# Storing the lower weight halves of block 0's projections in DRAM and loading them in the three later blocks

## The chip, the cores and the metric

The kernel runs on one core of a Trainium2 chip. The metric is the device time of one execution in microseconds; below that is the median of the runs shown. A profiled execution has its own time, which stands beside its span.

## The reference, cut to what matters

One hybrid decoder layer over 2048 tokens of width 1024 (float32), with 16 learned meta tokens ahead of them:

```
h    = rmsnorm(x, norm1_g)
proj = h @ w_in                       # all input projections at once
dq, dk, dv, dz, db, da, gq, gk, gv, gr, glr = split(proj)
o_dn  = gated_delta_chunked(conv+silu of dq, dk, dv, ...)   # 4 heads, chunk by chunk, a state is carried
o_gla = gla_chunked(gq, gk, gv, ...)                        # 4 heads, the same
x = x + concat(o_dn, o_gla gated and normed) @ w_out
x = x + square(relu(rmsnorm(x) @ w_up)) @ w_down
return rmsnorm(x)
```

What the change touches is `h @ w_in`, made once for each block of 512 tokens with the same `w_in`.

## The kernel before, in words

**Products of float32 from three passes.** An operand is split into an upper half `hi` (the value rounded to the matmul's own format, by ScalarE) and a lower half `lo = value - hi` (by VectorE or GpSimd). `mm3` (L116 to L120) then makes three matmuls into one PSUM bank: upper by upper (L118), and the two products of an upper and a lower half (L119, L120). Nothing is kept of a lower half between blocks: each block splits the same weights anew.

**A chunk of weights.** `wchunk` (L96) loads a raw chunk `wraw` of 128 x 2 x n from DRAM (L98, three buffers), casts it to `whi` on ScalarE (L102, two buffers) and subtracts to get `wlo` (L103, two buffers). In the projections the subtraction of chunks 1 and 2 of each group of four is on GpSimd, that of chunks 0 and 3 on VectorE. n is 512 for `wch` and 390 for `wtk`.

**The projections, `phase_a(b)`.** There are four blocks of 512 tokens (b = 0 to 3). A block has eight groups, in this order: `wtk` 0, `wch` 0 to 2 (keys, queries and values, with a convolution after each), `wch` 3, `wtk` 1 to 3. Each group has four chunks of 24 matmuls: 32 chunks and 768 matmuls a block, besides small products for the meta tokens in block 0. The tokens' operand comes from `xk` (L185), split into `hh` and `hl` (L113, L114). Results leave PSUM through VectorE and ScalarE and go to DRAM (`qkv_d`, `gla_d`, `gate_d`, `gv_d`).

**The scan.** `ahead(b)` runs at the middle of phase_a(b): four `dn_pre` (L481, each loads a `kqv` tile, three buffers) and `dn_inverse` (L559, a chain of small VectorE steps on `inv_v`, which goes through DRAM on both sides). `scan_chunk` carries the state: a GLA part (`gla`) and a delta part (`dn_levels`, `dn_rec`, which loads `kqv` as well). Scan chunks of block b stand between the projection matmuls of block b+1, so TensorE has independent work while a chain of the scan waits. Block 0 has no scan before it. After the projections come the output projection (`wo_block`) and the MLP (`layer1`, `layer2`), which the change doesn't touch.

**What sets the order.** The program is written once, and a scheduler with priorities orders the instructions of each engine; each engine then takes its own list strictly in order and waits on semaphores. All loads and stores are issued by one queue, SP's, in its order, so what waits there holds all behind it. A transfer also waits until the one that was issued eight before it has landed (the lanes DMAHW0 to DMAHW7 in the rows below). Pools fix how many buffers a name has; a load into a buffer waits for the last reader of what was there.

`k4` tiles (L72) are 4 KB a partition, four buffers, for statistics and decays.

Of the kernel before, what the change touches and what calls it, by code (L numbers as in the profile page):

```python
# [8 lines left out]
F32 = mybir.dt.float32  # L9
F32R = mybir.dt.float32r  # L10
I32 = mybir.dt.int32
AF = mybir.ActivationFunctionType
ALU = mybir.AluOpType
# [3 lines left out]
D = 1024  # L17
# [24 lines left out]
def hybrid_kernel(ctx: ExitStack, tc: tile.TileContext, I: dict, out: bass.AP):  # L42
    nc = tc.nc
    V, A, G, T = nc.vector, nc.scalar, nc.gpsimd, nc.tensor

    cp = ctx.enter_context(tc.tile_pool(name="const", bufs=1))
    dp = ctx.enter_context(tc.tile_pool(name="scratch", bufs=1, space=DRAM))
    mmp = ctx.enter_context(tc.tile_pool(name="mmp", bufs=4, space=PSUM))
    wp = ctx.enter_context(tc.tile_pool(name="wts", bufs=2))
    wstack = ctx.enter_context(ExitStack())  # L50
    wk = wstack.enter_context(tc.tile_pool(name="work", bufs=2))
# [11 lines left out]
    def mm(name):  # L63
        return mmp.tile([128, 512], F32, name=name, tag="mm")
# [5 lines left out]
        return wk.tile([128, 512], F32, name=name, tag="t512", bufs=4)  # L70

    def k4(name, q=wk):  # L72
        return q.tile([128, D], F32, name=name, tag="k4", bufs=4)

    def av(name, dt=F32, q=wk):
        return q.tile([128, TB + 4], dt, name=name, tag="av", bufs=8)
# [16 lines left out]
    mhalf = const("mhalf", [128, 16])  # L93
    G.memset(mhalf, -0.5)

    def wchunk(src, n, q=wp, eng=V):  # L96
        raw = wp.tile([128, 2, 512], F32, name="wraw", tag="wr", bufs=3)
        nc.sync.dma_start(out=raw[:, :, 0:n], in_=src)  # L98
        hi = q.tile([128, 2, 512], F32R, name="whi", tag="wh")
        lo = q.tile([128, 2, 512], F32R, name="wlo", tag="wl")  # L100
        with tc.high_priority(offset=HP):
            A.copy(out=hi[:, :, 0:n], in_=raw[:, :, 0:n])  # L102
            eng.tensor_tensor(  # L103
                out=lo[:, :, 0:n], in0=raw[:, :, 0:n], in1=hi[:, :, 0:n].bitcast(F32), op=ALU.subtract
            )
        return raw, hi, lo

    def split(src, hi, lo, scale=None):
# [23 lines left out]
    xs_d = [dp.tile([128, NK, TB], F32, name=f"xs_d{b}") for b in range(NB)]  # L132
    rb_d = [dp.tile([128, TB], F32, name=f"rb_d{b}") for b in range(NB)]
    sq_d = [dp.tile([128, 16, TB], F32, name=f"sq_d{i}") for i in range(7)]


    scan = ctx.enter_context(ExitStack())
    bps = scan.enter_context(tc.tile_pool(name="bps", bufs=4, space=PSUM))
    bp = scan.enter_context(tc.tile_pool(name="scan", bufs=1, side="right"))

    def ps(name):
        return bps.tile([128, 512], F32, name=name, tag="ps")
# [16 lines left out]
    def phase_a(b, kc, late=None, mid=None):  # L159
        convw, tails, g1, ealog, dtb, w2, gb, rmask = kc  # L160
        meta = b == 0
# [19 lines left out]
        def normless(k):  # L181

            if k not in hT:
                xk = t512("xk")
                nc.sync.dma_start(out=xk, in_=I["xT"][b, k])  # L185
                hT[k] = act("h")
                split(xk, *hT[k], g1[:, k : k + 1])
            return hT[k]
# [4 lines left out]
        if meta:  # L193
# [6 lines left out]
                out=hm[:, :, 0:NMETA], in0=hm[:, :, 0:NMETA], in1=g1.unsqueeze(2).broadcast_to([128, NK, NMETA]), op=ALU.mult  # L200
# [36 lines left out]
        def step(between):  # L237

            for job in list(stages):
                if between or not job[1]:  # L240
                    job[1] = next(job[0], None)
                    if job[1] is None:
                        stages.remove(job)

        def group(src, n, chan, evac, on_done, meta_n=0, on_meta=None, mid=None):
            banks = [mm("pa") for _ in range(4)]
            pm = ps("pmeta") if meta_n else None
            mh = meta_n // 2
            for kk in range(4):
                raw, wh, wl = wchunk(src[kk], n, eng=G if kk in (1, 2) else V)  # L250
                for j in range(4):
                    for k2 in range(2):
                        k = 2 * kk + k2
                        js = slice(j * 128, (j + 1) * 128)
                        h = normless(k)
                        w = (wh[:, k2, 0:n], wl[:, k2, 0:n])
                        if chan:
                            mm3(banks[j], [x[:, js] for x in w], h, k == 0, k == NK - 1)
                        else:
                            mm3(banks[j][:, 0:n], [x[:, js] for x in h], w, k == 0, k == NK - 1)  # L260
                step(False)
                for q in range(4 if meta_n else 0):
                    half, k2 = divmod(q, 2)
                    T.matmul(
                        pm[32 * q : 32 * q + 32, 0:mh],
                        lhsT=hm[:, 2 * kk + k2, :],
                        rhs=raw[:, k2, half * mh : (half + 1) * mh],
                        start=kk == 0,
                        stop=kk == 3,
                    )  # L270
            if mid is not None:
                mid()
            if meta_n:
                sb = k4("msb")
                V.tensor_copy(out=sb[:, 0:mh], in_=pm[:, 0:mh])
                po = ps("pmeta2")
                if chan:
                    for j in range(4):
                        c0 = j % 2 * 128
                        T.matmul(  # L280
                            po[:, j * NMETA : (j + 1) * NMETA], lhsT=sb[:, c0 : c0 + 128], rhs=eq[:, j // 2, :], start=True, stop=True
                        )
                else:
                    for half in range(2):
                        T.matmul(po[0:NMETA, half * mh : (half + 1) * mh], lhsT=eq[:, half, :], rhs=sb[:, 0:mh], start=True, stop=True)
                on_meta(po)
            st = [evac(j, banks[j]) for j in range(4)]
            step(True)
            for j in range(4):
                on_done(j, st[j])  # L290
# [190 lines left out]
    def dn_pre(c):  # L481
# [3 lines left out]
        gcb = b2k("gcb", "gcb", 2)  # L485
        if c is not None:
            b, t = divmod(c, 4)
            kqv = bp.tile([128, 12, 128], F32, name="kqv", tag="kqv", bufs=3)
            nc.sync.dma_start(out=kqv[:, 0:8, :], in_=qkv_d[b][:, 0:8, t * 128 : (t + 1) * 128])
            load_gcb(gcb, c)  # L490
            bt, gc = beta[b][:, t, :], gct[b][:, t, :]
        else:
            kqv = kqv_m
            load_gcb(gcb, c)
            bt, gc = beta_m[:, 0, :], gct_m[:, 0, :]
# [25 lines left out]
        if c is not None:  # L521
# [13 lines left out]
            out=gm[:p, :, 0:p], in0=gcb[:p, :, 0:p], in1=madd[:p, 0:p].unsqueeze(1).broadcast_to([p, 4, p]), op=ALU.add  # L535
# [7 lines left out]
        for h in range(4):  # L543
            V.scalar_tensor_tensor(
                out=U[:p, h, 0:p], in0=h4(pkk)[:p, h, 0:p], scalar=nbrk2[:p, h : h + 1], in1=gm[:p, h, 0:p], op0=ALU.mult, op1=ALU.mult
# [108 lines left out]
    def dn_rec(r, gate, mix, first):  # L654
# [2 lines left out]
        load_gcb(gcb, c)  # L657
        if c is not None:
            b, t = divmod(c, 4)
            kqv = bp.tile([128, 12, 128], F32, name="kqv", tag="kqv", bufs=3)  # L660
            nc.sync.dma_start(out=kqv, in_=qkv_d[b][:, :, t * 128 : (t + 1) * 128])
            at, kdt = b2k("at", "at", 1), b2k("kdt", "kdt", 1)
            nc.sync.dma_start(out=at, in_=at_d[c])
            nc.sync.dma_start(out=kdt, in_=kdt_d[c])
        else:
            kqv, kdt = kqv_m, r["kdt"]
# [31 lines left out]
        else:  # L698
            for h in range(4):
                V.scalar_tensor_tensor(  # L700
                    out=S[:, h, :], in0=S[:, h, :], scalar=egc[:, h, p - 1 : p], in1=h4(pu)[:, h, :], op0=ALU.mult, op1=ALU.add
# [761 lines left out]
```

## Time and profile before

| | before |
|---|---|
| median of 3 runs | 2676.49 us (2676.47 to 2682.16) |
| profiled execution: its time, its span | 2689.82 us, 2688.0 us |
| TensorE busy | 2468.2 us (92%) |
| VectorE busy | 1900.8 us (71%) |
| ScalarE busy | 1145.8 us (43%) |
| GpSimd busy | 498.0 us (19%) |
| moved by DMA | 477.81 MB, 178 GB/s on the mean |
| mean granted TensorE clock | 0.954 |

Rows of the profile name an engine, a line of the kernel, the operation, and the tiles out<-in. "PE" is TensorE, "PEld" its weight loads, "DVE" VectorE, "ACT" ScalarE, "POOL" GpSimd, "SPq" the queue that issues transfers. In the table of stretches each row is a stretch of the span in microseconds with its length, the busy time of each engine and its number of instructions in brackets, then the granted TensorE clock, the mean busy share of the 16 DMA engines and GB/s. In a row of waits stand the waiting engine and line, what it waited for, the microseconds in total, the number of times and the longest.

### The profile page before, as it was taken

How to read it: one execution, taken by the hardware profiler on the slowest of the kernel's cores; microseconds unless marked ns; L12 is line 12 of the kernel's file. 1: busy time of each engine (PE TensorE's matmuls, PEld its weight loads, DVE VectorE, ACT ScalarE, POOL GpSimd, SP SyncE). 2: the span in 40 equal slices, each digit the busy share in tenths (PEclk: the TensorE clock that was granted, in tenths of full speed). 3: DMA queues.
4: the chain of work that ended last, by engine and by line, in shares of the span. 5: the costliest groups of instructions: out<-in, count | busy, mean ns of one | idle time of the engine just before them, and what ended most of it. 6: DMA issues, size and time to landing. Idle time of an engine off the chain costs nothing.

```text
span 2688.0 us, 36763 instructions
## 1 busy us (share of the span) xinstructions
PE 2468.2 (92%) x12810; PEld 2034.4 (76%) x12810; DVE 1900.8 (71%) x3405; ACT 1145.8 (43%) x2243; POOL 498.0 (19%) x380
## 2 busy tenths in 40 slices
PE   8958999899989997996999999999969999899997
PEld 6747878777877786775778887778757888788776
DVE  4857788679787968667666666677778666557765
ACT  3334444434543454334444454443354444444433
POOL 2122233333332341111011110000111111100002
PEclk9979999899999998997999999999989999999998
DMA  5266546745674468653444447667527444656644
GB/s 174 91 197 193 160 153 198 226 151 177 200 218 148 160 202 288 197 166 108 147 141 159 143 147 264 206 217 226 165 91 249 166 144 151 209 187 210 214 136 134
DMA packets 304074, 477.81 MB, mean 178 GB/s; under 512 B 44545, under 2 KB 147537, under 8 KB 303889
## 3 DMA queue, kind: packets, MB, share of 16 engines
q1 hardware_dynamic: 303888, 475.48, 54.6%
q8 instruction: 100, 1.64, 0.2%
q14 instruction: 86, 0.70, 0.1%
HBM read 341.12 MB, written 134.26 MB: 177 GB/s over the span
## 4 chain that ended last, share of the span: by engine, by line
PE 52%; DVE 7%; DMA 3%; issue 1%; ACT 1%; SPq 1%; POOL 0%; DVEq 0%; POOLq 0%; ACTq 0%
PE p L119 15%; PE p L118 15%; PE p L120 15%; PE pc L120 2%; PE pc L118 2%; PE pc L119 1%; DMA br<-sq_d 1%; DVE bl L983 1%; DVE b L954 0%; DVE wlo L103 0%; DMA gcb<-gcr_d 0%; DMA xr<-xs_d 0%; DMA gl<-gla_d 0%; SPq L592 0%; DMA mixk<-mix_d 0%
## 5 line engine op out<-in xcount | busy, mean ns | idle before, releaser
L119 PE MATMUL p<-bl,w7h 128*128 128x512 f32 x832 | 325.5, 401 | 9.3 <-DVE bl L983 9.3
L120 PE MATMUL p<-bh,w7l 128*128 128x512 f32 x832 | 320.1, 398 | 0.0
L982 ACT CAST w7h<-s 128x1024 fp32r<-128x1024 f32 (+1 forms) x128 | 120.5, 942 | 346.6 <-PE p L119 287.9
L118 PE MATMUL p<-bh,w7h 128*128 128x512 f32 x832 | 228.9, 403 | 14.9 <-ACT bh L982 12.7
L102 ACT CAST whi<-wraw 128x1024 fp32r<-128x1024 f32 (+1 forms) x160 | 154.6, 967 | 205.9 <-PE pa L119 77.8
L118 PE MATMUL pa<-hh,whi 128*128 128x512 f32 x512 | 210.6, 412 | 9.9 <-DVE craw L424 4.6
L983 DVE TENSOR_TENSOR w7l<-s,w7h 128x1024 fp32r<-128x1024 f32 (+1 forms) x128 | 140.0, 1094 | 94.8 <-ACT w7h L982 90.5
L103 POOL TENSOR_TENSOR wlo<-wraw,whi 128x780 fp32r<-128x780 f32 (+1 forms) x64 | 144.2, 2254 | 338.5 <-ACT whi L102 281.4
L119 PE MATMUL pa<-hl,whi 128*128 128x512 f32 x512 | 206.6, 404 | 0.0
L118 PEld LDWEIGHTS p<-bh,w7h 128*128 128x128 f32 x832 | 159.4, 192 | 54.8 <-ACT bh L982 13.9
L120 PE MATMUL pa<-hh,wlo 128*128 128x512 f32 x512 | 196.4, 404 | 1.9 <-DVE wlo L103 1.5
L119 PEld LDWEIGHTS p<-bl,w7h 128*128 128x128 f32 x832 | 158.4, 190 | 49.5 <-DVE bl L983 11.5
L983 DVE TENSOR_TENSOR w7l<-w,w7h 128x1024 fp32r<-128x1024 f32 (+1 forms) x96 | 102.0, 1062 | 128.1 <-ACT w7h L982 124.3
L118 PE MATMUL pa<-whi,hh 128*128 128x390 f32 x512 | 173.7, 361 | 17.9 <-ACT hh L113 17.5
L119 PE MATMUL pa<-wlo,hh 128*128 128x390 f32 x512 | 182.2, 357 | 6.3 <-DVE wlo L103 4.2
L120 PEld LDWEIGHTS p<-bh,w7l 128*128 128x128 f32 x832 | 157.9, 190 | 37.8
L120 PE MATMUL pa<-whi,hl 128*128 128x390 f32 x512 | 177.0, 350 | 0.0
L983 DVE TENSOR_TENSOR bl<-br,bh 128x1024 fp32r<-128x1024 f32 (+2 forms) x144 | 149.2, 1038 | 32.1 <-ACT bh L982 31.9
L982 ACT CAST bh<-br 128x1024 fp32r<-128x1024 f32 (+2 forms) x144 | 123.2, 855 | 85.0 <-PE p L120 48.1
L103 DVE TENSOR_TENSOR wlo<-wraw,whi 128x1024 fp32r<-128x1024 f32 (+1 forms) x96 | 114.4, 1192 | 62.1 <-ACT whi L102 61.6
L1083 POOL TENSOR_TENSOR q<-r 128x512 f32<-128x512 f32 x32 | 58.5, 1829 | 521.4 <-ACT r L1082 479.2
L891 POOL TENSOR_TENSOR tot<-tot,sqk 128x512 f32<-128x512 f32 (+1 forms) x28 | 37.9, 1354 | 625.7 <-ACT sqk L890 624.5
(380 smaller groups left out, 6232.7 us busy)
## 6 DMA issues: line engine op xcount, KB each, us to landing
br<-sq_d SPq DMA_DIRECT2D x208, 256.0 KB
w<-in_dn_dram SPq DMA_DIRECT2D x96, 512.0 KB
wraw<-in_wch_dram SPq DMA_DIRECT2D x64, 512.0 KB
w<-in_up_dram SPq DMA_DIRECT2D x64, 512.0 KB
sq_d<-q SPq DMA_DIRECT2D x128, 256.0 KB
wraw<-in_wtk_dram SPq DMA_DIRECT2D x64, 390.0 KB
sq_d<-c SPq DMA_DIRECT2D x96, 256.0 KB
wraw<-in_wo_dram SPq DMA_DIRECT2D x32, 512.0 KB
```

The costliest lines, as they stand in the source:

```text
L102: A.copy(out=hi[:, :, 0:n], in_=raw[:, :, 0:n])
L103: eng.tensor_tensor(out=lo[:, :, 0:n], in0=raw[:, :, 0:n], in1=hi[:, :, 0:n].bitcast(F32), op=ALU.subtract)
L118: T.matmul(o, lhsT=ah, rhs=bh, start=first, stop=False)
L119: T.matmul(o, lhsT=ah, rhs=bl, start=False, stop=False)
L120: T.matmul(o, lhsT=al, rhs=bh, start=False, stop=last)
L891: eng.tensor_tensor(out=tot, in0=tot, in1=sq, op=ALU.add)
L982: A.copy(out=hi, in_=x)
L983: V.tensor_tensor(out=lo, in0=x, in1=hi.bitcast(F32), op=ALU.subtract)
L1083: G.tensor_tensor(out=q12, in0=u, in1=r5, op=ALU.add)
```

## The change

In block 0 each lower half is made as before and then also stored to DRAM, in 32 new tiles `lo_d`. In blocks 1 to 3 the subtraction is gone and `wlo` is loaded from `lo_d`; the raw chunk is still loaded, because ScalarE still casts the upper half from it. A third buffer for `wlo` (tag `wl3`) is used by every third chunk of a block. Two pools give up room for it: `k4` goes from four buffers to three and `kqv` from three to two. All transfers are issued by SP.

The numbers: 32 stores in block 0 and 96 loads in blocks 1 to 3, half of them of 512 KB and half of 390 KB; 48 subtractions go from VectorE and 48 from GpSimd.

```
-        return q.tile([128, D], F32, name=name, tag="k4", bufs=4)
+        return q.tile([128, D], F32, name=name, tag="k4", bufs=3)
...
-    def wchunk(src, n, q=wp, eng=V):
+    def wchunk(src, n, q=wp, eng=V, save=None, saved=None, third=False):
         raw = wp.tile([128, 2, 512], F32, name="wraw", tag="wr", bufs=3)
         nc.sync.dma_start(out=raw[:, :, 0:n], in_=src)
         hi = q.tile([128, 2, 512], F32R, name="whi", tag="wh")
-        lo = q.tile([128, 2, 512], F32R, name="wlo", tag="wl")
+        if third:
+            lo = wk.tile([128, 2, 512], F32R, name="wlo", tag="wl3", bufs=1)
+        else:
+            lo = q.tile([128, 2, 512], F32R, name="wlo", tag="wl")
+        if saved is not None:
+            nc.sync.dma_start(out=lo[:, :, 0:n].bitcast(F32), in_=saved[:, :, 0:n])
         with tc.high_priority(offset=HP):
             A.copy(out=hi[:, :, 0:n], in_=raw[:, :, 0:n])
-            eng.tensor_tensor(
-                out=lo[:, :, 0:n], in0=raw[:, :, 0:n], in1=hi[:, :, 0:n].bitcast(F32), op=ALU.subtract
-            )
+            if saved is None:
+                eng.tensor_tensor(
+                    out=lo[:, :, 0:n], in0=raw[:, :, 0:n], in1=hi[:, :, 0:n].bitcast(F32), op=ALU.subtract
+                )
+        if save is not None:
+            nc.sync.dma_start(out=save[:, :, 0:n], in_=lo[:, :, 0:n].bitcast(F32))
         return raw, hi, lo
...
+    lo_d = [[dp.tile([128, 2, 512], F32, name=f"lo_d{i}{k}") for k in range(4)] for i in range(8)]
...
             for kk in range(4):
-                raw, wh, wl = wchunk(src[kk], n, eng=G if kk in (1, 2) else V)
+                d = lo_d[gi][kk]
+                raw, wh, wl = wchunk(src[kk], n, eng=G if kk in (1, 2) else V, **{"save" if meta else "saved": d}, third=(4 * gi + kk) % 3 == 2)
...
-            kqv = bp.tile([128, 12, 128], F32, name="kqv", tag="kqv", bufs=3)
+            kqv = bp.tile([128, 12, 128], F32, name="kqv", tag="kqv", bufs=2)
```

`gi` counts the groups of a block from 0 to 7, and the last hunk stands in both `dn_pre` and `dn_rec`.

The rows of an engine's list below are in its order; what stands in brackets is what the instruction waits for (a DMAHW lane is a transfer issued earlier). In the changed kernel L99 is the raw load, L106 the load of a lower half, L114 its store, L196 the load of `xk`, L375 the store of the gates and L505 the load of `kqv` in `dn_pre`.

GpSimd in block 1, between the scan's products `kg` and `qg` and the next ones, before:

```order
L677 TENSOR_TENSOR kg<-kqv,egc 128x512 [waits Activation_49]
L678 TENSOR_TENSOR qg<-kqv,egc 128x512
L103 TENSOR_TENSOR wlo<-wraw,whi 128x1024 [waits DMAHW5_49,PE_49,Activation_49]
L103 TENSOR_TENSOR wlo<-wraw,whi 128x1024 [waits DVE_49,PE_49,DMAHW3_49,Activation_49,Pool_49]
L103 TENSOR_TENSOR wlo<-wraw,whi 128x1024 [waits DVE_49,DMAHW4_49,PE_49,Activation_49]
L90 TENSOR_TENSOR f_r<-f_u,mhalf 128x4 [waits DVE_49]
L766 TENSOR_TENSOR kd<-gl,dl 128x2x64 [waits DMAHW0_49,PE_49]
```

And now:

```order
L90 TENSOR_TENSOR f_r<-f_u,mhalf 128x4 [waits DVE_49]
L693 TENSOR_TENSOR kg<-kqv,egc 128x512 [waits Activation_49]
L694 TENSOR_TENSOR qg<-kqv,egc 128x512
L90 TENSOR_TENSOR f_r<-f_u,mhalf 128x4 [waits DVE_49,Pool_49]
L782 TENSOR_TENSOR kd<-gl,dl 128x2x64 [waits DMAHW3_49,PE_49]
```

The scan's own small steps (`f_r`, `kd`) now follow one another with no subtraction between them.

SP at the start of block 1, where the first `xk` of the block is loaded, before:

```order
L98 DMA wraw<-in_wtk_dram 128x2x390 [waits Pool_49] x2
L98 DMA wraw<-in_wtk_dram 128x2x390 [waits DVE_49]
L98 DMA wraw<-in_wtk_dram 128x2x390 [waits DMAHW7_49,DMAHW2_49,DVE_49]
L359 DMA gate_d_82<-gth 128x390 [waits DMAHW3_49,DVE_49]
L359 DMA gate_d_82<-gth 128x390 [waits DMAHW4_49,DVE_49]
L359 DMA gate_d_82<-gth 128x390 [waits DMAHW5_49,DVE_49]
L847 DMA gate<-gate_d_82 128x512 [waits DMAHW6_49,DMAHW3_49]
L185 DMA xk<-in_xT_dram 128x512
```

And now:

```order
L106 DMA wlo<-lo_d_163 128x2x390 [waits DMAHW2_49,DMAHW0_49,PE_49]
L99 DMA wraw<-in_wtk_dram 128x2x390 [waits DMAHW1_49,Activation_49]
L375 DMA gate_d_82<-gth 128x390 [waits DVE_49]
L106 DMA wlo<-lo_d_164 128x2x390 [waits DMAHW3_49,PE_49]
L106 DMA wlo<-lo_d_165 128x2x390 [waits DMAHW4_49]
L375 DMA gate_d_82<-gth 128x390 [waits DMAHW5_49,DVE_49]
L375 DMA gate_d_82<-gth 128x390 [waits DMAHW6_49,DVE_49]
L375 DMA gate_d_82<-gth 128x390 [waits DMAHW7_49,DVE_49]
L99 DMA wraw<-in_wtk_dram 128x2x390 [waits DMAHW0_49,Activation_49]
L99 DMA wraw<-in_wch_dram 128x1024 [waits DMAHW1_49,Activation_49]
L863 DMA gate<-gate_d_82 128x512 [waits DMAHW2_49]
L196 DMA xk<-in_xT_dram 128x512 [waits DMAHW3_49]
```

A raw load now waits only for ScalarE's cast, no longer for a subtraction. A load of a lower half waits for TensorE, and two of them and two raw loads have come between the first gate store of this stretch and the load of `xk`.

SP in the middle of block 0, where the four `dn_pre` load their `kqv`, before:

```order
L489 DMA kqv<-qkv_d_74 128x8x128 [waits DMAHW3_49]
L489 DMA kqv<-qkv_d_74 128x8x128 [waits DMAHW4_49]
L440 DMA qkv_d_74<-cy 128x512 [waits DMAHW5_49,DVE_49]
L440 DMA qkv_d_74<-cy 128x512 [waits DVE_49]
L477 DMA gcb<-gcr_d_90 128x512 [waits Pool_49]
L489 DMA kqv<-qkv_d_74 128x8x128 [waits DMAHW2_49,PE_49]
```

And now:

```order
L505 DMA kqv<-qkv_d_74 128x8x128 [waits DMAHW4_49,PE_49]
L493 DMA gcb<-gcr_d_90 128x512 [waits Pool_49]
L570 DMA u_d_99<-U 128x512 [waits DMAHW5_49,DVE_49]
L570 DMA at_d_115<-at 128x512 [waits DMAHW6_49,DVE_49]
L570 DMA kdt_d_132<-kdt 128x512 [waits DMAHW7_49,DVE_49]
L456 DMA qkv_d_74<-cy 128x512 [waits DMAHW0_49,DVE_49]
L505 DMA kqv<-qkv_d_74 128x8x128 [waits DMAHW1_49,PE_49]
```

Before, one of the four `kqv` loads waited for TensorE; now the last two do, and the last one also stands behind stores of the first `dn_pre`'s results.

## The prediction on record

> **What bounds the kernel now.** I read the page's busy times first, then the table of stretches with cuts between the blocks, then TensorE's waits in blocks 1 to 3, which alone lose the subtractions. The page's first rows:
>
> ```profile
> span 2688.0 us, 36763 instructions
> PE 2468.2 (92%) x12810; PEld 2034.4 (76%) x12810; DVE 1900.8 (71%) x3405; ACT 1145.8 (43%) x2243; POOL 498.0 (19%) x380
> ```
>
> The stretches are block 0, the projections of blocks 1, 2 and 3 with the scan among them, and the end of the scan with most of the output projection; the MLP follows:
>
> ```profile
> core 0: us, PE busy (x) PEld busy (x) DVE busy (x) ACT busy (x) POOL busy (x), PEclk, DMA share, GB/s
> 0.00:215.00 215.00, 175.79 (x918) 136.77 (x919) 137.94 (x327) 74.87 (x190) 49.46 (x39) 0.89 0.48 156
> 215.00:475.00 260.00, 240.84 (x1478) 210.40 (x1476) 201.65 (x451) 115.80 (x297) 83.68 (x67) 0.95 0.58 178
> 475.00:735.00 260.00, 237.18 (x1504) 203.51 (x1504) 205.83 (x457) 110.15 (x287) 85.44 (x64) 0.95 0.59 184
> 735.00:1015.00 280.00, 259.95 (x1707) 224.62 (x1705) 222.69 (x502) 122.68 (x340) 94.40 (x72) 0.98 0.60 184
> 1015.00:1320.00 305.00, 255.50 (x1515) 209.34 (x1514) 208.93 (x434) 119.25 (x250) 39.50 (x41) 0.89 0.56 183
> ```
>
> TensorE is busy 738.0 of 800 us in blocks 1 to 3 (the sum of three rows), so all that any change to the other engines can give back there is 62 us of idle time, and what the clock loses around it: the granted clock is 0.96 on the mean of the three, some 32 us of full speed. VectorE is busy 630.2 of 800 us (79%), GpSimd 263.5 (33%). What TensorE waited for between 215 and 1015 us:
>
> ```profile
> PE pa L118 <- ACT hh L113: 11.2, 1, 11.2
> PE py L685 <- DVE nkv L682: 8.3, 3, 4.2
> PE pkk L541 <- DVE U L544: 4.9, 4, 2.7
> PE pp L618 <- ACT rt L613: 4.6, 1, 4.6
> ...
> PE pa L119 <- DVE wlo L103: 4.2, 2, 2.8
> ...
> PE pa L119 <- POOL wlo L103: 2.1, 2, 1.2
> ...
> PE pa L120 <- DVE wlo L103: 1.5, 2, 1.2
> ...
> PE pgla L335 <- DVE gqk L390: 1.1, 1, 1.1
> ...
> PE pa L120 <- POOL wlo L103: 0.5, 2, 0.2
> ```
>
> The lower halves themselves are waited for 8.3 us in all. The other rows released by VectorE from `nkv` (8.3) down to `gqk` (1.1) are eleven and come to 33 us: steps of the scan and of the evacuation that come late because VectorE's list is full. The kernel is bound by TensorE; this change can only take away waits.
>
> **The change part by part.** *Work removed.* The subtractions of blocks 1 to 3 stand in this stretch:
>
> ```profile
> core 0: us, PE busy (x) PEld busy (x) DVE busy (x) POOL busy (x), PEclk, DMA share, GB/s
> 215.00:1015.00 800.00, 311.52 (x843) 163.24 (x842) 62.22 (x53) 116.78 (x52) 0.96 0.59 182
> ```
>
> These are the instructions on `wlo`; 53 and 52 of them are in the window, 48 and 48 go (the rest are the tail of block 0 and the start of the output projection), so 56 us of VectorE and 108 us of GpSimd, at 1.17 and 2.25 us each. VectorE falls to (630 - 56)/800 = 72%, GpSimd to 19%.
>
> *The waits on lower halves.* Of the 8.3 us, one of 1.2 us lies in block 0's tail; 7 us go. The costliest is followed by a slow stretch of the clock:
>
> ```profile
> 763.41 0.69 PE L119 MATMUL pa<-wlo,hh 128*128 128x390 f32 x1 [2.76 <-DVE wlo L103]
> ```
>
> ```profile
> 760.00:765.00 5.00, 2.24 (x9) 1.91 (x8) 2.69 (x9) 0.36 (x1) 0.00 (x0) 0.75 0.79 208
> 765.00:770.00 5.00, 5.00 (x40) 4.51 (x39) 4.83 (x11) 4.50 (x11) 2.54 (x2) 0.57 0.43 126
> ```
>
> After a gap of 2.76 us the clock is at 0.75 and 0.57 for two slices of 5 us: (0.25 + 0.43) x 5 = 3 us more. So a short gap costs about its own length again. The Trainium skill (TensorE: Matmul & The Clock Gate, Part 1: The HAM clock gate) has the clock halved after at least one idle window of about 3.4 us; by that a gap of 2.76 us would cost nothing more, and the sum below would be some 7 us smaller (the 3 here and the 4 of the next part). The rows here speak against it, and I go by them.
>
> *Waits on VectorE's other steps, 33 us.* VectorE has 9% less to do. It is also held up less: GpSimd's long operations stretch short ones of VectorE, as these two rows show, where a copy of three columns takes 159 ns at the median and 2372 at most, and a step that follows one of GpSimd's has a median of 1215 and a least value of 150.
>
> ```profile
> L430 DVE COPY tails<-craw x48: 147/159/2372, 62.2 to 905.7; 128x3 f32<-128x3 f32 x48
> L515 DVE TENSOR_TENSOR nkh<-nkh,rk_r x17: 150/1215/1825, 152.1 to 1006.7; 128x4 f32<-128x4 f32 x16, 16x4 f32<-16x4 f32 x1
> ```
>
> An estimate: with the load from 79% to about 70%, waits in a list would shrink by between nothing (they are chains, each step waits for the step before it) and 38% (if waits go as load over free time: 0.79/0.21 against 0.70/0.30), that is by 0 to 13 us. I take 7, the middle, since the rows hold both chains (`nkv`, `U`) and late evacuations (`craw`, `gqk`). With the clock's share, about 0.5 for each microsecond of gap (32 us lost beside 62 us idle), 4 us more.
>
> *Loads added.* 96 loads of 390 or 512 KB. Each waits for TensorE to be done with the chunk three before it, as the order of SP's list and the three buffers have it, so it is issued some two chunks before its use: two times 24 matmuls at 0.35 to 0.4 us, 17 to 19 us. A load of 512 KB took about 4 us to its user here:
>
> ```profile
> 138.94 2.01 SPq L489 DMA_DIRECT2D kqv<-qkv_d  x3
> ```
>
> ```profile
> 142.96 1.08 PE L498 MATMUL pk<-ident,kqv 128*128 128x128 f32 x4 [4.20 <-DMA kqv<-qkv_d]
> ```
>
> So the loads themselves are covered four times over. Queued behind each are the other transfers of SP's list; counting SP's list against TensorE's at that price a matmul, only the `xk` of block 1 is needed within 5 us after such a gate. The chunks' lead covers the load; if it were gone, each would cost up to 4 us. In return the raw loads no longer wait for a subtraction on VectorE:
>
> ```profile
> SPq L98 <- DVE wlo L103: 74.7, 28, 6.8
> ```
>
> *The start of block 1.* The 11.2 us on `hh` begin when block 0's last matmul ends and hold until `xk` has landed and been cast. In the new list two loads of lower halves and two raw loads stand among the gate stores ahead of it. An issue of 390 KB takes 0.55 us:
>
> ```profile
> L98 SPq DMA_DIRECT2D wraw<-in_wtk_dram x64: 540/546/1951, 1.2 to 978.3; - x64
> ```
>
> ```profile
> 265.00:275.00 10.00, 7.60 (x34) 7.31 (x35) 4.24 (x6) 4.89 (x8) 0.00 (x0) 0.70 0.85 267
> ```
>
> That is at most 4 x 0.55 = 2 us of issue, and 1.6 MB more on the way with `xk`, which at the 267 GB/s of the second row take 6 us. Between 0 (the gate stores ahead wait for VectorE anyway) and 6 us; I take +3.
>
> *Block 0.* 32 stores of at most 0.55 us of issue, 18 us, spread over 215 us with the DMA engines busy 0.48; each waits for its subtraction, and the raw load behind it is needed about two chunks later, so nothing on the path. With two `kqv` buffers the last of four `dn_pre` gets its tile only after the second is through TensorE, which has nothing else to do there, so each microsecond counts:
>
> ```profile
> 148.31 0.37 SPq L489 DMA_DIRECT2D kqv<-qkv_d  x1
> ```
>
> ```profile
> 155.79 2.08 PE L550 MATMUL pqk<-kqv 128*128 128x128 f32 x8 [3.22 <-DVE U L544]
> ...
> 162.34 0.60 PE L498 MATMUL pk<-ident,kqv 128*128 128x128 f32 x4
> ```
>
> Before, the fourth tile was issued at 148.31 and used at 162.34; now its load follows the second `dn_pre`'s last matmul (row L550, which ends at 157.9), and 4 us for it leave it at about 162. I take +2, between 0 and 8 (two loads in full).
>
> *Fuller DMA.* (16 x 512 + 16 x 390) KB = 14.4 MB a block more, on 182 GB/s x 267 us = 49 MB: from 0.59 to about 0.76 of the engines. Most transfers have lead; those at the inverse don't. +4, between 0 and 20.
>
> *The rest.* From 1015 us on the same instructions run; at most the order shifts by a few places: 0, within 5 either way.
>
> The sum against the profiled execution's 2689.8 us (span 2688.0): -7 - 3 - 7 - 4 + 3 + 2 + 4 = -12. That execution lies 13 above the median of 2676.5; the same difference on the median gives 2664.5.
>
> **The rivals.** *No change:* VectorE's steps are late because their chains are, and only the 7 + 3 us of lower halves go, against +9 of costs: 2676. For it: `nkv` and `U` are steps of chains, TensorE is already 92% busy. Against: `craw` and `gqk` are plain evacuations, and wait only for their turn.
>
> *Slower: bursts of DMA at the inverse.* In each block `dn_inverse` reads and writes `inv_v` through DRAM while `kqv`, the statistics' `xt` and raw chunks are loaded. In two slices the rate was at what looks like a ceiling:
>
> ```profile
> 755.00:760.00 5.00, 5.00 (x43) 4.70 (x42) 1.27 (x5) 0.85 (x1) 1.16 (x2) 1.00 1.01 358
> 780.00:785.00 5.00, 5.00 (x23) 4.82 (x22) 3.85 (x8) 1.24 (x2) 0.00 (x0) 0.70 1.06 356
> ```
>
> There VectorE stands for `inv_v` with all its list behind it. SP's new list has four lower halves among a block's `inv_v` loads and two right behind: six of 390 KB are 2.3 MB, 6.6 us at 357 GB/s. If that goes straight to TensorE in three blocks, it is 20 us and 10 of clock, against the gain of 21 and with the 5 of block 0 and block 1's start: +14, 2690.5. It decides from about 5 us a block that pass to TensorE. For it: the share of 1.01 and 1.06 leaves no room there. Against: the stretches are short, the mean is 0.59. The Trainium skill (DMA: Bandwidth & Descriptors, Specifications) gives about 358 GB/s as a core's limit at HBM, which is what these two slices show.
>
> That the change doesn't do what it says I exclude: GpSimd's list has lost the rows.
>
> **How the numbers follow.** No difference within 0.2% (5.4 us), about what a measurement of this kernel can tell, counts as the same. Forecast (faster, by some 12): 0.58. Same: 0.20. Slower: 0.22, the bursts 0.15, an order of the scan that fits worse 0.07. The prediction is 2664.5. The low end takes VectorE's relief at its bound (-13 and -7 of clock) and half of the costs, 2651, and 2650 with a little of the shift after 1015 us; the high end reaches into the bursts, 2686. Left out are gains beyond the bounds and the worst of the bursts, 2 in 10 together.
>
> **What would show it.** Right: GpSimd busy near 390 and VectorE near 1830 us on the page, no row of TensorE waiting for `wlo` between 215 and 1015 us, its VectorE rows together nearer 25 than 33 us, a granted clock of 0.97 there. The wait on `hh` at block 1's start between 11 and 17 us. Wrong: TensorE waiting on transfers of `wlo`, `inv_v`, `kqv` or `U` in rows that weren't there, VectorE's rows at 33 us or more, or a time above 2682.

## The result, and the profile after

The changed kernel takes 2657.76 us (median of four runs, 2653.23 to 2660.84); the kernel before, 2678.56 (median of four runs, 2676.47 to 2682.16). The ratio is 0.992, with a 95% interval from 0.9898 to 0.9941: 20.8 us faster, where 2664.5 us was forecast. The profiled execution took 2655.41 us, span 2653.5; before's took 2689.82. These two lie 34.4 us apart, because before's is 11 above its median and after's 2 below. Where single profiles are set side by side below, differences of some 5 us mean nothing: the last part of the program, the MLP, in which nothing differs, took 1351 to 1359 us in the profiles of this study.

The first rows of the page of after:

```profile
span 2653.5 us, 36884 instructions
PE 2458.0 (93%) x12810; PEld 2030.0 (77%) x12810; DVE 1783.3 (67%) x3357; ACT 1146.9 (43%) x2243; POOL 379.4 (14%) x332
```

GpSimd is at 379 (390 was expected). VectorE is at 1783 where 1830 was expected: it lost 117.5 us, and the 48 subtractions that it no longer makes are only 56 of them.

The table of stretches of after, with the cuts that the prediction used:

```profile
0.00:215.00 215.00, 177.47 (x927) 138.52 (x927) 139.47 (x334) 75.75 (x182) 52.15 (x38) 0.90 0.61 206
215.00:475.00 260.00, 236.49 (x1506) 206.22 (x1505) 166.00 (x443) 117.02 (x311) 53.26 (x54) 0.96 0.77 251
475.00:735.00 260.00, 249.93 (x1631) 218.83 (x1630) 179.41 (x470) 120.11 (x321) 51.93 (x55) 0.96 0.81 260
735.00:1015.00 280.00, 256.72 (x1691) 221.99 (x1690) 187.19 (x503) 119.35 (x320) 45.69 (x51) 0.94 0.77 248
1015.00:1320.00 305.00, 270.90 (x1519) 221.44 (x1518) 214.00 (x408) 126.59 (x250) 37.44 (x40) 0.92 0.52 173
```

The DMA engines went from 0.59 to 0.77 or 0.81 of their time in blocks 1 to 3, as reckoned (0.76). The projections now end 25 us earlier, which these two rows show by the last start of such a matmul, of before and then of after:

```profile
L119 PE MATMUL pa<-wlo,hh x512: 336/341/695, 7.8 to 1014.7; 128*128 128x390 f32 x171
```

```profile
L128 PE MATMUL pa<-wlo,hh x512: 336/341/695, 7.9 to 989.4; 128*128 128x390 f32 x171
```

So the stretch from 215 to 990 us of after does the work of 215 to 1015 us of before. Of before, and then of after:

```profile
215.00:1015.00 800.00, 737.97 (x4686) 638.54 (x4684) 630.16 (x1409) 348.62 (x921) 263.52 (x203) 0.96 0.59 182
```

```profile
215.00:990.00 775.00, 725.65 (x4710) 631.80 (x4711) 515.00 (x1363) 349.29 (x932) 148.50 (x158) 0.96 0.78 251
```

TensorE stands idle 49 us instead of 62, and is busy 12 us less for about as many instructions. The rest of the profiles' difference, some 9 us, lies between 990 and 1296 us, before the MLP. What TensorE waits for in after between 215 and 1015 us:

```profile
PE pa L127 <- ACT hh L122: 14.9, 1, 14.9
PE pr L646 <- DVE wt L638: 13.0, 4, 5.9
PE pk L514 <- DMA kqv<-qkv_d: 6.4, 3, 2.3
PE py L701 <- DVE nkv L698: 5.3, 3, 3.6
...
PE pa L129 <- DMA wlo<-lo_d: 4.3, 2, 2.7
...
PE pa L128 <- POOL wlo L110: 1.7, 1, 1.7
...
PE pa L128 <- DVE wlo L110: 0.4, 1, 0.4
```

The first of these, at the start of block 1, stands so in the timeline of before, and then of after (start, duration, instruction, and in brackets the idle time ahead of it):

```profile
267.40 0.69 PE L118 MATMUL pa<-whi,hh 128*128 128x390 f32 x1 [11.23 <-ACT hh L113]
```

```profile
270.62 0.69 PE L127 MATMUL pa<-whi,hh 128*128 128x390 f32 x1 [14.93 <-ACT hh L122]
```

`craw`, the plain evacuation, which had been waited for in several rows, is gone from the list; `hh` has grown by 3.7 us, a step of the scan, `wt`, has gone from 3.3 to 13.0, and two rows name transfers, `kqv` and `wlo`. The row of `kqv` is not the loads' alone: the pools alone, with no transfer added, have 3.9 us of it. The waits on loads of lower halves stand where the rival of the bursts placed them, at the inverse of blocks 2 and 3. The slices around the costlier of the two:

```profile
800.00:805.00 5.00, 3.83 (x30) 2.80 (x30) 0.71 (x1) 1.05 (x1) 0.13 (x1) 1.00 0.61 166
805.00:810.00 5.00, 2.34 (x19) 1.71 (x14) 0.00 (x0) 1.14 (x3) 2.55 (x3) 0.62 0.99 350
810.00:815.00 5.00, 5.00 (x17) 3.94 (x17) 2.91 (x8) 0.72 (x1) 0.00 (x0) 0.69 0.71 287
```

SP issued the stores of `inv_v` and the load of `U` until 802 us and only then six weight loads, three of them lower halves; they filled the DMA engines (0.99, 350 GB/s), TensorE stood 2.7 us and the clock fell to 0.62 and 0.69. The rival was real, at 4.3 us of waits on lower halves in all instead of 20.

### The profile page after: what moved, and what is told of

The parts are those of the page before. It is cut to its first block, busy times and chain, and to the rows that moved or that the text cites. A ratio compares the mean times of both kernels' runs of the same rounds, so it can differ in the third digit from the quotient of the medians.

```text
span 2653.5 us, 36884 instructions
## 1 busy us (share of the span) xinstructions
PE 2458.0 (93%) x12810; PEld 2030.0 (77%) x12810; DVE 1783.3 (67%) x3357; ACT 1146.9 (43%) x2243; POOL 379.4 (14%) x332
## 5 line engine op out<-in xcount | busy, mean ns | idle before, releaser
L129 PE MATMUL pa<-hh,wlo 128*128 128x512 f32 x512 | 202.3, 403 | 4.3 <-DMA wlo<-lo_d 4.3
L127 PEld LDWEIGHTS p<-bh,w7h 128*128 128x128 f32 x832 | 159.6, 192 | 55.0 <-ACT bh L998 13.7
L998 ACT CAST w7h<-w 128x1024 fp32r<-128x1024 f32 (+1 forms) x96 | 86.7, 904 | 146.8 <-PE p L128 144.5
L1099 POOL TENSOR_TENSOR q<-r 128x512 f32<-128x512 f32 x32 | 58.4, 1825 | 521.1 <-ACT r L1098 482.1
L129 PEld LDWEIGHTS pa<-hh,wlo 128*128 128x128 f32 x512 | 97.3, 190 | 29.7 <-DMA wlo<-lo_d 5.0
```

Of the source, the lines that this page charges most:

```text
L127: T.matmul(o, lhsT=ah, rhs=bh, start=first, stop=False)
L129: T.matmul(o, lhsT=al, rhs=bh, start=False, stop=last)
L998: A.copy(out=hi, in_=x)
L1099: G.tensor_tensor(out=q12, in0=u, in1=r5, op=ALU.add)
```

## The experiments

At the outset the theory was that of the prediction: the gain is VectorE's relief, and the transfers take some of it back. Its rivals were the waits on lower halves alone, the third buffer alone, and GpSimd's long operations as the thing that had held VectorE up. All medians are against runs of the kernel before on the same chip in the same batch, which gave 2678.4 to 2679.0 us.

**The pools alone.** The changed kernel with neither `save` nor `saved`:

```
-                raw, wh, wl = wchunk(src[kk], n, eng=G if kk in (1, 2) else V, **{"save" if meta else "saved": d}, third=(4 * gi + kk) % 3 == 2)
+                raw, wh, wl = wchunk(src[kk], n, eng=G if kk in (1, 2) else V, third=(4 * gi + kk) % 3 == 2)
```

> The pools of the changed kernel alone (three k4, two kqv buffers, a third wlo buffer for every third chunk), with every subtraction kept and nothing stored or loaded. If the gain comes from lighter lists of VectorE and GpSimd: no gain here, the kernel before plus 0 to 8 us for the fourth kqv tile of block 0 (2678 to 2687). If the third buffer of the lower halves is what brings it (chunks split earlier): 10 us or more below the kernel before, 2668 or less.

2681.31 us, ratio 1.0006 (0.9995 to 1.0018). The third buffer and the smaller pools together change nothing that is clear of the noise; what each does alone was not measured.

**GpSimd's half alone, VectorE's half alone.** The same call, here for the first of the two; the second has `(0, 3)` in the last condition.

```
-                raw, wh, wl = wchunk(src[kk], n, eng=G if kk in (1, 2) else V, **{"save" if meta else "saved": d}, third=(4 * gi + kk) % 3 == 2)
+                raw, wh, wl = wchunk(src[kk], n, eng=G if kk in (1, 2) else V, **({"save" if meta else "saved": d} if kk in (1, 2) else {}), third=(4 * gi + kk) % 3 == 2)
```

> Only the lower halves of chunks 1 and 2, which GpSimd makes, are stored and loaded (16 stores, 48 loads); VectorE keeps its 48 subtractions. If VectorE's steps come earlier because GpSimd's long operations no longer hold it up: most of the 21 us, 2666 or less, with VectorE's busy time down by 50 us or more though it executes the same instructions. If VectorE's own subtractions are what counts: at most 7 us, 2671 or more. If only the waits on lower halves count: GpSimd's 2 to 3 us of them, 2675.

> Only the lower halves of chunks 0 and 3, which VectorE makes, are stored and loaded (16 stores, 48 loads); GpSimd keeps its 48 subtractions. If VectorE's own subtractions are what counts: most of the 21 us, 2666 or less, and VectorE's busy time down by 57 us. If GpSimd's holding up of VectorE is what counts: at most 7 us, 2671 or more. If only the waits on lower halves count: VectorE's 5 to 6 us and some clock, 2671.

GpSimd's half gives 2639.96 us, 0.9857 (0.9844 to 0.987): half of the change brings 38.5 us, nearly twice what the whole brings. VectorE's half gives 2665.61, 0.9954 (0.9941 to 0.9966). The page of the first:

```profile
span 2636.3 us, 36823 instructions
...
PE 2440.4 (93%) x12810; PEld 2019.2 (77%) x12810; DVE 1833.2 (70%) x3405; ACT 1146.2 (43%) x2243; POOL 384.5 (15%) x332
```

VectorE executes as many instructions as before (3405) and is busy 68 us less. That is what the rival said. The halves do not add up (38.5 and 13 against 21), so something is lost when both are there.

**The transfers alone.** Everything is stored and loaded, but the loads go to a tile without a reader:

```
-            nc.sync.dma_start(out=lo[:, :, 0:n].bitcast(F32), in_=saved[:, :, 0:n])
+            spare = wk.tile([128, 2, 512], F32, name="spare", tag="wl3", bufs=1)
+            nc.sync.dma_start(out=spare[:, :, 0:n], in_=saved[:, :, 0:n])
...
-            if saved is None:
-                eng.tensor_tensor(
+            eng.tensor_tensor(
...
-                raw, wh, wl = wchunk(src[kk], n, eng=G if kk in (1, 2) else V, **{"save" if meta else "saved": d}, third=(4 * gi + kk) % 3 == 2)
+                raw, wh, wl = wchunk(src[kk], n, eng=G if kk in (1, 2) else V, **{"save" if meta else "saved": d})
```

> All 32 stores and 96 loads, but the loads go into a tile that nothing reads, and every subtraction is still made, in two buffers as before. This prices the transfers alone, with the pools of the changed kernel. By the prediction's terms (two kqv buffers 2, start of block 1 3, fuller DMA 4): 9 us above the kernel before, 2688. If the DMA had free room for them: 0 to 3 us, as the pools alone. If bursts at the inverse count: 14 us or more above, 2693 or more.

2687.98 us, 1.0041 (1.0026 to 1.0056): 9.5 us above before, of which 6.7 above the kernel with the pools alone. The prediction's 9 is met to the microsecond, for transfers beside subtractions that are still made; but not term by term, since 3 of the 9 were for a longer wait on `hh` at the start of block 1, and that wait is 11.1 us here and was 11.2 before.

**No transfers and no subtractions.** One lower half stands for all of blocks 1 to 3, in all chunks or in GpSimd's only:

```
+    keep = []
...
-            lo = q.tile([128, 2, 512], F32R, name="wlo", tag="wl")
-        if saved is not None:
-            nc.sync.dma_start(out=lo[:, :, 0:n].bitcast(F32), in_=saved[:, :, 0:n])
+            lo = q.tile([128, 2, 512], F32R, name="wlo", tag="wl") if saved is None else saved
...
-            nc.sync.dma_start(out=save[:, :, 0:n], in_=lo[:, :, 0:n].bitcast(F32))
+            if n == 512 and not keep:
+                keep.append(wk.tile([128, 2, 512], F32R, name="keep", tag="wl3", bufs=1))
+                V.tensor_copy(out=keep[0], in_=lo.bitcast(F32))
...
-                raw, wh, wl = wchunk(src[kk], n, eng=G if kk in (1, 2) else V, **{"save" if meta else "saved": d}, third=(4 * gi + kk) % 3 == 2)
+                raw, wh, wl = wchunk(src[kk], n, eng=G if kk in (1, 2) else V, **{"save" if meta else "saved": d if meta else keep[0]})
```

The second has the same with `if kk in (1, 2)` for what is passed. Both leave out the third buffer of lower halves.

> Blocks 1 to 3 neither subtract nor load: one lower half, kept from block 0, stands for all of them (so their small products are left out of the right sum), and nothing is stored. What is left of the change is the relief of VectorE and GpSimd with no transfer at all. If the transfers of VectorE's half eat its gain: clearly below the 2640 of the kernel that loads GpSimd's half alone, 2630 or less. If VectorE's own subtractions bring nothing once GpSimd's are gone: 2632 to 2640, the same as the next kernel.

> As the kernel before it, but only GpSimd's chunks 1 and 2 of blocks 1 to 3 use the fixed lower half (their right products are left out); VectorE subtracts its 48 chunks. Nothing is stored or loaded. Against the kernel with the loads of GpSimd's half (2640) this prices 16 stores and 48 loads: half of the 9.5 us measured for all of them, so 2635, if transfers cost the same everywhere. If VectorE's own subtractions count: 10 us or more above the kernel with all lower halves fixed; if not, the same within 4.

2628.73 us, 0.9816 (0.9802 to 0.9829), and 2633.99, 0.9832 (0.9819 to 0.9846). Without transfers the change is worth 50 us, and 45 of them come with GpSimd's subtractions; VectorE's own 48 are worth 5 us more once GpSimd's are gone, which the intervals hardly part from nothing; what they are worth while GpSimd's are still there was not run without transfers. The transfers of GpSimd's half, with the third buffer that goes with them, cost 6.0 us (2639.96 against 2633.99).

**All subtractions on VectorE.** The kernel before with one word changed, and no transfer:

```
-                raw, wh, wl = wchunk(src[kk], n, eng=G if kk in (1, 2) else V)
+                raw, wh, wl = wchunk(src[kk], n, eng=V)
```

> The kernel before, with the subtractions of chunks 1 and 2 moved from GpSimd to VectorE; no store, no load. If GpSimd's long operations are what holds VectorE up: faster than before, 2650 to 2670, although VectorE now executes 64 more subtractions (75 us at 1.17 us each). If the number of VectorE's own operations is what counts: slower than before by 10 us or more, 2690 or above.

2637.59 us, 0.9847 (0.9833 to 0.986), beyond what either theory gave it: twice the gain of the change, without a store or a load. The page:

```profile
span 2634.1 us, 36801 instructions
...
PE 2446.9 (93%) x12810; PEld 2023.3 (77%) x12810; DVE 1871.2 (71%) x3469; ACT 1146.2 (44%) x2243; POOL 342.1 (13%) x316
```

VectorE makes 64 subtractions more than before and is busy 30 us less.

**GpSimd busy again.** The same kernel, but GpSimd makes the lower halves of chunks 1 and 2 as well, for no reader:

```
-    def wchunk(src, n, q=wp, eng=V):
+    def wchunk(src, n, q=wp, eng=V, spare=False):
...
+            if spare:
+                sp = wk.tile([128, 2, 512], F32R, name="spare", tag="spare", bufs=1)
+                G.tensor_tensor(
+                    out=sp[:, :, 0:n], in0=raw[:, :, 0:n], in1=hi[:, :, 0:n].bitcast(F32), op=ALU.subtract
+                )
...
-                raw, wh, wl = wchunk(src[kk], n, eng=V)
+                raw, wh, wl = wchunk(src[kk], n, eng=V, spare=kk in (1, 2))
```

> VectorE makes all lower halves, as in the kernel with all subtractions on VectorE (2638), and GpSimd makes those of chunks 1 and 2 once more, into a tile that nothing reads. So TensorE never waits for GpSimd's lower halves, but GpSimd's long operations are back. If these hold up VectorE and the scan's own steps on GpSimd: 25 us or more of the 41 are lost, 2663 or more, and VectorE's busy time rises by 80 us or more for the same instructions. If what counted was that GpSimd's lower halves came late: 2638 to 2645.

2696.17 us, 1.0057 (1.0039 to 1.0076): 58.6 us lost by operations whose results nobody uses. The page:

```profile
span 2687.0 us, 36887 instructions
...
PE 2461.7 (92%) x12810; PEld 2027.2 (75%) x12810; DVE 1964.7 (73%) x3469; ACT 1144.2 (43%) x2243; POOL 522.8 (19%) x380
```

For the same 3469 instructions VectorE is busy 93.5 us longer. Which of its steps are stretched can be read from groups of one line each, the least, the median and the longest duration in ns. In this kernel, a copy within SBUF and the evacuation of PSUM `craw`, which has one operand in PSUM:

```profile
L435 DVE COPY tails<-craw x48: 146/160/2340, 64.5 to 903.8; 128x3 f32<-128x3 f32 x48
```

```profile
L429 DVE TENSOR_TENSOR craw<-pa,rb x48: 673/684/693, 55.7 to 900.2; 128x512 f32<-128x512 f32 x48
```

The copy, in the kernel without the spare subtractions:

```profile
L430 DVE COPY tails<-craw x48: 125/159/1265, 63.1 to 857.4; 128x3 f32<-128x3 f32 x48
```

The longest goes from 1265 to 2340 ns, while the step that reads PSUM never strays from its median by more than 2%. The copy of 2340 ns ends with a spare subtraction, at 386.1 us (start, duration):

```profile
383.74 2.34 DVE L435 COPY tails<-craw 128x3 f32<-128x3 f32 x1
382.96 3.10 POOL L108 TENSOR_TENSOR spare<-wraw,whi 128x1024 fp32r<-128x1024 f32 x1 [16.07 <-ACT whi L102]
```

Each of the eight copies over 600 ns in this kernel (`tails<-craw` and `craw<-tails`) ends 20 to 28 ns after a GpSimd operation that ran beside it; without the spare subtractions there are four, beside `kg` and `qg`. The Trainium skill (SBUF — State Buffer, Who interferes with whom) states that a VectorE instruction with two SBUF inputs contends with a GpSimd instruction that reads SBUF, that one in a two-port mode and GpSimd block each other for a whole instruction, and that a VectorE instruction with at most one SBUF input outside these modes goes free. The trace agrees with it in the evacuation, which has one input in PSUM and stays at 693 ns, and in a step `nkh` with two SBUF inputs, shown further down; that the copy, with one SBUF input, ran in a two-port mode no view here shows.

Two other paths stand beside VectorE's holding up in this run: the scan's own steps queue behind the spare subtractions on GpSimd, and a raw buffer is held until they are through. Their rows are short. From 215 us to the end of the projections TensorE waits for VectorE 52 us in this kernel and 21 in the one without the spare subtractions, and for GpSimd in neither. VectorE itself waits for GpSimd 15.6 and 13.7 us, and ScalarE's casts wait for raw loads 12.2 and 10.2, though SP stands 26.5 us at raw loads for the spare subtractions. The largest of TensorE's rows released by VectorE, in this kernel and then without the spare subtractions:

```profile
PE pr L635 <- DVE wt L627: 10.2, 2, 5.3
PE pa L125 <- DVE wlo L103: 9.1, 7, 3.8
PE pa L124 <- DVE wlo L103: 6.5, 5, 2.0
```

```profile
PE pr L630 <- DVE wt L622: 7.0, 2, 5.2
PE pkk L541 <- DVE U L544: 4.6, 4, 1.7
PE pa L119 <- DVE wlo L103: 4.5, 1, 4.5
```

So the rows put the loss on VectorE's late steps; no run takes the other two paths away by themselves.

**The stores of VectorE's half.** GpSimd's half is stored and loaded, VectorE's only stored:

```
-                raw, wh, wl = wchunk(src[kk], n, eng=G if kk in (1, 2) else V, **({"save" if meta else "saved": d} if kk in (1, 2) else {}), third=(4 * gi + kk) % 3 == 2)
+                raw, wh, wl = wchunk(src[kk], n, eng=G if kk in (1, 2) else V, **({"save" if meta else "saved": d} if meta or kk in (1, 2) else {}), third=(4 * gi + kk) % 3 == 2)
```

> The kernel that loads GpSimd's half alone, with the lower halves of VectorE's chunks stored in block 0 as well (nobody loads them): the price of 16 stores. If stores sit in front of loads that block 0 needs: block 0 ends 6 us later, as it does in the changed kernel against the one with GpSimd's half (255.4 against 249.2 us), and a wait of 3 to 5 us on rstd_bc comes back; 2646. If the stores lie beside other work, as the prediction took them: 2640.

2653.42 us, 0.9907 (0.9893 to 0.9921): 13.5 us for 16 stores, twice the price expected, and not at the place. The start of block 1, in the kernel with GpSimd's half alone and then in this one:

```profile
265.78 0.69 PE L127 MATMUL pa<-whi,hh 128*128 128x390 f32 x1 [16.23 <-ACT hh L122]
```

```profile
267.52 0.69 PE L127 MATMUL pa<-whi,hh 128*128 128x390 f32 x1 [16.40 <-ACT hh L122]
```

Only 1.7 us are lost by then, though all the stores lie before it. The remainder comes later, where both kernels have the same transfers: the projections end at 976.8 us in the first profile and 983.5 in the second, and 5 of the 12.6 us between the two spans lie in the MLP, in which nothing differs. The two kernels' times do not overlap (at most 2643.66, at least 2650.64), so a loss is clear, but its size is less sure than the medians make it look.

**Stores issued later.** The changed kernel, each store behind the raw loads of the next two chunks:

```
+    due = []
...
+        if len(due) == 2 or save is None:
+            for o, i in due[: 1 if save is not None else 2]:
+                nc.sync.dma_start(out=o, in_=i)
+            del due[: 1 if save is not None else 2]
...
-            nc.sync.dma_start(out=save[:, :, 0:n], in_=lo[:, :, 0:n].bitcast(F32))
+            due.append((save[:, :, 0:n], lo[:, :, 0:n].bitcast(F32)))
```

> The changed kernel (2658), but each store of block 0 is issued two chunks later in the program, behind two more raw loads, when its subtraction has long been done. If SP held the loads behind stores that waited for a subtraction: the 13 us that VectorE's 16 stores cost come back, 2645. If the 13 us are the transfers themselves or another order of the work: no change, 2653 to 2662.

2656.93 us, 0.9908 (0.989 to 0.9926), no change. But the edit did not reach its aim. SP's waits at these stores in block 0, in this kernel:

```profile
SPq L104 <- POOL wlo L116: 27.2, 6, 10.6
SPq L104 <- DVE wlo L116: 19.2, 7, 5.2
```

In the changed kernel they are 26.4 and 16.0 us. SP runs ahead and stands there all the same, so this run decides nothing about it.

**The tokens' operand earlier.** All subtractions on VectorE, and `xk` of the next block loaded and split during the last group of a block:

```
...
+                if last and b + 1 < NB:
+                    normless(2 * kk, b + 1)
+                    normless(2 * kk + 1, b + 1)
...
```

> The kernel with all subtractions on VectorE (2638; no store, no load of lower halves), and the tokens' operand of the next block is loaded and split during the last group of a block, ahead of the gate stores. If the wait at block 1's start is the late load of it: the wait on hh of 7.6 us there goes, with its share of clock some 8 to 10 us in all, 2628. If the wait only moves (the split needs buffers that the last group still reads): 2638.

2622.04 us, 0.9781 (0.9762 to 0.9799), 15.6 below the kernel without it. The wait of 7.6 us on `hh` is gone (3.7 us for a cast of the weights stand near its place), and the projections, which end at 916 us, run nearly without a gap:

```profile
250.00:1000.00 750.00, 721.17 (x4679) 617.47 (x4678) 603.01 (x1431) 343.06 (x902) 140.47 (x148) 0.99 0.65 204
```

TensorE is busy 721 of 750 us at a clock of 0.99. In the changed kernel, whose projections reach to 990 us, it is, in the same stretch:

```profile
250.00:1000.00 750.00, 696.41 (x4558) 603.86 (x4557) 496.67 (x1310) 335.30 (x895) 135.71 (x148) 0.96 0.78 252
```

Part of it is given back behind the projections. From their end to that of the output projection's matmuls, in the kernel with all subtractions on VectorE and then in this one:

```profile
954.00:1278.00 324.00, 268.85 (x1625) 219.60 (x1625) 224.65 (x471) 125.86 (x269) 41.31 (x46) 0.89 0.56 183
```

```profile
916.00:1263.00 347.00, 289.12 (x1762) 237.36 (x1762) 239.63 (x526) 139.82 (x356) 53.05 (x54) 0.90 0.58 186
```

That takes 23 us more, with 137 more matmul instructions in it: work of the scan that the shorter projections no longer have among them.

**The scan's products on VectorE too.**

```
-            G.tensor_tensor(out=kg, in0=kqv[:, 0:4, :], in1=egc, op=ALU.mult)
-            G.tensor_tensor(out=qg, in0=kqv[:, 4:8, :], in1=egc, op=ALU.mult)
+            V.tensor_tensor(out=kg, in0=kqv[:, 0:4, :], in1=egc, op=ALU.mult)
+            V.tensor_tensor(out=qg, in0=kqv[:, 4:8, :], in1=egc, op=ALU.mult)
```

> As the kernel before it, with kg and qg (32 products of 128 by 512, 1.45 and 1.60 us on GpSimd) moved to VectorE as well. If any long operation on GpSimd costs more there than on VectorE: another 5 to 15 us, 2615 to 2623. If VectorE's load counts from here on (some 24 us more of work for it): slower than the kernel before it by up to 10 us.

2624.13 us, 0.9786 (0.9765 to 0.9807): the same within the noise. So neither reading of the expectation is shown; whether a gain and a loss cancel was not parted. The kernel before it is the fastest of the study, 57 us below before and 36 below the change.

## Why the prediction was right, and where not

The sign and the range held, and the time came out 7 us below the forecast (the gain 9 us above it, 20.8 against 12, since the kernel before measured 2 us more here); but two larger errors stood against each other, and that they nearly cancelled is luck.

*The gain was mis-sized, by the step that turned VectorE's load into waits.* The prediction had 7 us for lower halves, 3 for clock after them, 7 of relief and 4 of clock, 21 in all; without transfers the same relief is worth 50 us. Load over free time counted VectorE's own operations, and bounded the relief at 13 us. But VectorE's own subtractions are worth some 5 us once GpSimd's are gone; 45 come from taking GpSimd's away. The prediction had named the holding up and had the row for it (`tails`, 159 ns at the median and 2372 at most), and then gave it hardly a price: 1900.8 less the 56 removed is 1845, and it took 1830, so 15 us of busy time. 1783 was measured, which is 61 beyond the 56. Its second row, the step of 1215 ns after one of GpSimd's, does show a holding up, but mostly by an operation that the change leaves in place. In the kernel with neither subtractions nor `kg` and `qg` on GpSimd the median is the same, and such a step ends with GpSimd's `gm`, here within 0.03 us:

```profile
L518 DVE TENSOR_TENSOR nkh<-nkh,rk_r x17: 145/1215/1244, 138.2 to 969.9; 128x4 f32<-128x4 f32 x16, 16x4 f32<-16x4 f32 x1
```

```profile
440.23 1.24 DVE L518 TENSOR_TENSOR nkh<-nkh,rk_r 128x4 f32<-128x4 f32 x1 [0.60 <-POOL rk_r L90]
440.16 1.28 POOL L537 TENSOR_TENSOR gm<-gcb,madd 128x512 f32<-128x512 f32 x1
```

In the kernel before, only the two longest of the 17, 1825 and 1802 ns, stand beside a subtraction.

*The costs were mis-sized too.* 9 us were taken, and 9.5 measured with the transfers beside all the old work. In the change itself they are 29 (2657.76 against 2628.73, a kernel in which TensorE has no lower half to wait for in blocks 1 to 3). The steps by which the kernels differ, taken in this order: VectorE's 48 subtractions 5.3, GpSimd's stores and loads 6.0, VectorE's stores 13.5, and 4.3 more when VectorE's loads take the place of its subtractions. So VectorE's half of the change makes the kernel some 18 us slower (2657.76 against 2639.96), though its subtractions are worth 5 where nothing is transferred and GpSimd's are gone. While GpSimd's are still there the same half gains 13. Why the medians put 13.5 on 16 stores, most of it after the last of them, stays open: another order of the later work was not tried by itself, and the run that was to take SP's waits at the stores away left them there.

*The waits on lower halves* went, as taken (only 1.7 and 0.4 us remain in block 0's tail), but 4.3 us came back as waits on their loads, where the prediction had said none.

*The start of block 1*: +3 taken, +3.7 measured, but not for the reason given. The prediction had four loads queued ahead of `xk`. The kernel with the pools alone and the one with GpSimd's lower halves fixed have none of them and wait no less, while the one with all the transfers beside the old work waits 11.1 us:

```profile
PE pa L127 <- ACT hh L122: 16.8, 1, 16.8
```

```profile
PE pa L129 <- ACT hh L124: 17.0, 2, 16.4
```

So the agreement of this term is luck, and its cause is open. *Block 0*: +2 taken; its last projections end where they did (the gap before block 1 starts at 256.2 us before and 255.7 after). *The bursts* are there, at two inverses, a fifth of the size that would have turned the result.

*The signs it named* came out mixed. TensorE's rows released by VectorE came to 27 us between 215 and 1015 us (nearer 25 than 33, as for right), almost half of it the row of `wt`; that row has 14.4 us in the kernel with GpSimd's lower halves fixed, where nothing is transferred, so the transfers are not shown as its cause. But rows on transfers of `wlo` and `kqv`, which it had named as signs of being wrong, appeared as well, 4.3 and 6.4 us.

*The clock* did not show: 0.97 was expected between 215 and 1015 us, and it is 0.95 there and 0.96 over the same work, as before. 12 us less busy time is under 2%, which two digits cannot show.

*The rest*: 0 within 5 was taken after 1015 us; the profiles differ by some 9 there, in two single executions whose medians lie 14 us closer together than they do, so no cause is given.

## What to carry to other kernels

When two engines share a kind of work, price the second engine by what it does to the first: run the kernel with all of it on one engine, before storing anything in DRAM. A saving that is made of two halves should be tried by halves; here one half carried the gain and the other cost more than it brought. A total that comes out right says little of its terms: only the runs without transfers showed that gain and cost were both some 20 to 30 us too small.

## What the runs showed of the hardware

GpSimd's subtractions stretch VectorE's steps by more than they relieve it of: 64 of them made the same VectorE instructions 93.5 us longer in all, while 64 subtractions on VectorE itself take 75 (an estimate, at the 1.17 us of the kernel before). It is not the subtractions alone: `kg`, `qg` and `gm` hold VectorE up in the same way (645 to 1265 ns for the copies, up to 1244 for `nkh`). And it works both ways: in the changed kernel GpSimd's own 16 took 1824 ns at least, where no VectorE step ran beside it, 2353 at the median, and 6717 at most, beside a dozen of VectorE's steps:

```profile
L110 POOL TENSOR_TENSOR wlo<-wraw,whi x16: 1824/2353/6717, 9.2 to 241.7; 128x780 fp32r<-128x780 f32 x8, 128x1024 fp32r<-128x1024 f32 x8
```

The 5-us slice that holds a gap of 2.66 us on TensorE and the slice behind it show a clock of 0.62 and 0.69, as 0.75 and 0.57 stood at the gap of 2.76 us in the kernel before.
